# Down products of a SwiGLU block: from plain blocks to Strassen's seven products

## The chip, the cores and the metric

One core of one Trainium2 chip runs the whole block in one launch. TensorE (PE in the profile) multiplies, VectorE (DVE), ScalarE (ACT) and GpSimd (POOL) work on whole tiles, and SyncE (SP) issues the DMAs. Each engine takes its instructions in a fixed order and waits on semaphores. The metric is the device time of one execution in microseconds (us). The kernel before takes 2565.43 us, the median of 3 runs (2564.19 to 2566.57).

## The reference

One decoder block on 1024 tokens of width 1024: an input projection, sparse attention and a Mamba-2 mixer side by side, a merge with an output projection, and then a SwiGLU feed-forward of width `D_FF` = 2816, in float32. The change is in the last part:

```python
h = rms_norm(x, norm2_w[l]) * (1.0 + sc2) + sh2
x = x + gt2 * ((jax.nn.silu(h @ w_gate[l]) * (h @ w_up[l])) @ w_down[l])
return rms_norm(x, norm_f_w)
```

## The kernel before

A float32 product is made of three matmuls in a rounded format (`mm3k`, L292 to L297): every operand is split into a high part (a rounded copy, made by ACT) and a low part (operand minus high part, made by DVE or POOL), and high times high, high times low and low times high are summed in PSUM. One such step on 128 rows, 128 columns and 512 moving columns is three matmuls 128x512.

**Stages.** Startup and projections; the attention with the remaining input projections as fill between its steps (`background`, tiles `fps`); the SSD scan; the output projection; gate and up (`gate_up`, tiles `gu`); down (`down`, tiles `dps`); and the final norm. A `Flow` object (L105 to L211) sets the order at build time: each piece of work is queued with its needs and an assumed cost, and an engine takes the first of its queue whose needs are met by the assumed times. The chip then runs these orders as they are.

**Gate and up** already go by Strassen's scheme (Winograd's form, seven block products in place of eight): the tokens are cut in two halves (even and odd groups of 128), the inner width in two halves, and a block `b` of 256 columns of w_gate or w_up in two halves; there are 11 such blocks. `ff_sums` (L1814) puts the seven products of a block together on DVE; silu is ACT's, the product of gate and up POOL's (L1886), and `store_act` writes the result, 128 columns by 512 tokens, to DRAM (L1892).

**Down** runs in two halves `h` of the tokens. In each, eight PSUM banks hold the output (4 token tiles by 2 column halves), and for each of 22 slices `f` of the inner width `down_load` brings 128 rows of w_down (512 KB) and 256 KB of act, splits them (three pieces, `part`, L1693 ACT and L1695 DVE or POOL), and 8 steps of three matmuls follow: 2 x 22 x 8 = 352 steps. The w_down rows are loaded and split in both halves. Twelve pieces and 18 rows of 128x512 are shared; loads go three slices ahead. When a bank is full, DVE multiplies it by the gate vector (L1966) and adds it to the residual `x2` (L1969), ACT sums the squares (`square`, L1983), and `final` (L1987) makes the root on DVE (L1990 and the small steps L259 to L269), scales, and stores. In the second half the last three slices run bank by bank, so that the banks end one after the other:

```python
jobs = [(f, t, c) for f in range(NFF - LAST * h) for t in range(4) for c in range(2)]
if h:
    jobs += [(f, t, c) for t in range(4) for c in range(2) for f in range(NFF - LAST, NFF)]
```

Of the kernel before, what the change touches and what calls it, by code (L numbers as in the profile page):

```python
# [19 lines left out]
D = 1024  # L20
# [11 lines left out]
WD_BUFS = {"ml": 1, "x1t": 8, "sl": 1}  # L32
# [207 lines left out]
class Kern:  # L240
# [316 lines left out]
    def projections(self):  # L557
# [20 lines left out]
        self.gst = {2: [], 5: []}  # L578
        self.ck = None
# [513 lines left out]

    def load_fill(self, n):
# [8 lines left out]
    def background(self):  # L1103
# [75 lines left out]
        for n, (kd, b) in enumerate(self.order):  # L1179
# [234 lines left out]
    def tail(self):  # L1414
# [6 lines left out]
        self.actd = self.dr.tile([NFF, 128, 1024], F, name="actd")  # L1421
# [266 lines left out]
    def part(self, p, src, need, lo_eng):  # L1688
# [129 lines left out]
    def ff_sums(self, s, p, q, b, ps, op):  # L1818
# [60 lines left out]
        for m, h, nm in ready:  # L1879
# [4 lines left out]
            else:  # L1884
# [3 lines left out]
                self.store_act(g, e, 2 * b + m, h)  # L1888

    def store_act(self, g, e, f, h):  # L1890
        A, V, G, D = self.ops()
        self.acts[f][h] = e = D(0.73, [e], lambda: self.nc.sync.dma_start(self.actd[f, :, 512 * h:512 * h + 512], g.t))  # L1892
        g.until(e)

    def down_load(self, h, f):
# [3 lines left out]
        raw = self.buf("raw", [128, 2, 512], f"wd{h}{f}")  # L1899
        d = D(1.46, [raw], lambda: nc.sync.dma_start(raw.t.rearrange("p a c -> p (a c)"), self.a["w_down"][128 * f:128 * f + 128]))  # L1900
        ws = []
        k4 = lambda x: x.rearrange("p (k c) -> p k c", c=128)
        for c in range(2):
            p = self.piece()
            ws.append((p, self.part(p, lambda c=c: k4(raw[:, c]), d, "VG"[c])))
        raw.until(*[w[1] for w in ws])
        x, p = self.row(), self.piece()
        d = D(0.73, [self.acts[f][h], x], lambda: nc.sync.dma_start(x.t, self.actd[f, :, 512 * h:512 * h + 512]))
        e = self.part(p, lambda: k4(x.t), d, "V")
        x.until(e)  # L1910
        return (p, e), ws

    def down_start(self):

        self.dl = {}
        self.dnext = [(h, f) for h in range(2) for f in range(NFF)]
        self.down_more()

    def down_more(self):
        if self.dnext and self.acts[self.dnext[0][1]][self.dnext[0][0]] is not None:  # L1920
            h, f = self.dnext.pop(0)
            self.dl[h, f] = self.down_load(h, f)

    def down(self):

        nc, a = self.nc, self.a
        A, V, G, D = self.ops()
        self.x2 = x2 = self.buf("h32", [128, NT, 1024], "x2")
        gn = self.buf("h32", [128, 2, 1024], "gn")
        x2op = []  # L1930

        for h in range(2):
            self.down_more()
        g2op = D(1.46, [gn] + self.gst[5], lambda: nc.sync.dma_start(gn[:, 0], self.gtd[1]))
        nfop = D(1.46, [gn], lambda: nc.sync.dma_start(gn[:, 1], a["norm_f_w"].partition_broadcast(128)))
        LAST = 3
        for h in range(2):
            banks = {}
            for n in range(8):
                t, c = divmod(n, 2)  # L1940
                banks[t, c] = self.buf(("s", "mm", "t", "o", "s", "mm", "t", "s")[n], [128, 512], "dps")
            jobs = [(f, t, c) for f in range(NFF - LAST * h) for t in range(4) for c in range(2)]
            if h:
# [406 lines left out]
```

## Time and profile before

| | us |
|---|---|
| median of 3 runs | 2565.43 |
| profiled execution | 2557.07 |
| its span, first to last instruction | 2555.3 |
| PE busy in the span | 2467.0 (97%) |
| down: first to last `dps` matmul starts | 2294.4 to 2540.1 |
| after the last matmul, to the end of the span | about 15 |

The span is what the trace shows; what lies around it is 1.8 us. A busy PE is back to back with matmuls; an engine's idle time counts only where the PE, or at the end the last store, waits for it. Times of instructions are those of this one execution.

### The profile page before, as it was taken

How to read it: one execution, taken by the hardware profiler on the slowest of the kernel's cores; microseconds unless marked ns; L12 is line 12 of the kernel's file. 1: busy time of each engine (PE TensorE's matmuls, PEld its weight loads, DVE VectorE, ACT ScalarE, POOL GpSimd, SP SyncE). 2: the span in 40 equal slices, each digit the busy share in tenths (PEclk: the TensorE clock that was granted, in tenths of full speed). 3: DMA queues.
4: the chain of work that ended last, by engine and by line, in shares of the span. 5: the costliest groups of instructions: out<-in, count | busy, mean ns of one | idle time of the engine just before them, and what ended most of it. 6: DMA issues, size and time to landing. Idle time of an engine off the chain costs nothing. (4 is left out here: it accounts for less than half of the span.)

```text
span 2555.3 us, 39172 instructions
## 1 busy us (share of the span) xinstructions
PE 2467.0 (97%) x13806; PEld 2108.4 (83%) x13806; DVE 1698.1 (66%) x3887; ACT 1221.9 (48%) x2614; POOL 992.9 (39%) x792
## 2 busy tenths in 40 slices
PE   5999999999999999999999999999989999999997
PEld 5999879899888898988877777779968888888886
DVE  7644887877776678765477786777875555543555
ACT  4421766666556666654556446422642322323332
POOL 2111473635362636263443432101364544542222
PEclk8999999999999999999999999999999999999999
DMA  7433332213133323132456675336222322336352
GB/s 248 131 122 102 117 90 77 75 51 105 49 91 122 110 69 100 48 99 77 132 165 218 223 233 190 114 113 225 95 80 65 95 83 71 95 104 243 120 198 79
DMA packets 226261, 308.02 MB, mean 121 GB/s; under 512 B 17417, under 2 KB 151305, under 8 KB 225553
## 3 DMA queue, kind: packets, MB, share of 16 engines
q1 hardware_dynamic: 226064, 305.52, 37.4%
q8 instruction: 109, 1.79, 0.3%
q14 instruction: 88, 0.71, 0.1%
HBM read 229.83 MB, written 75.63 MB: 120 GB/s over the span
## 5 line engine op out<-in xcount | busy, mean ns | idle before, releaser
L2106 POOL TENSOR_SCALAR P<-P,sm,gate 128x640 f32<-128x640 f32 (+7 forms) x256 | 215.2, 852 | 369.3 <-DVE sm L2103 292.8
L2177 DVE TENSOR_TENSOR kv<-tp,kv 128x512 fp32r<-128x512 f32 (+1 forms) x296 | 189.5, 657 | 117.0 <-ACT kv L2176 115.5
L2176 ACT ACTIVATE kv<-tp 128x512 fp32r<-128x512 f32 (+1 forms) x296 | 164.8, 573 | 190.4 <-PE tp L2173 183.9
L2097 ACT ACTIVATE P<-P,sm 128x640 f32<-128x640 f32 (+7 forms) x256 | 186.8, 732 | 46.5 <-DVE sm L2093 43.6
L1068 PE MATMUL o<-kv 128*128 128x512 f32 x528 | 188.8, 409 | 12.7 <-DVE kv L2177 11.3
L2088 PE MATMUL S<-kv,Q 128*128 128x384 f32 (+5 forms) x768 | 182.6, 336 | 3.5 <-DVE sm L2093 3.4
L2093 DVE CUSTOM_DVE_ANT_0 P<-S,kb 128x256 f32<-128x256 f32 (+5 forms) x256 | 120.4, 494 | 59.6 <-PE tp L2173 31.4
L1827 DVE TENSOR_TENSOR ex<-ex,gu 128x512 f32<-128x512 f32 x117 | 79.0, 684 | 121.6 <-PE gu L297 110.0
L295 PE MATMUL fps<-hT_hi,whi_x 128*128 128x512 f32 x384 | 157.8, 411 | 0.0
L2173 PE MATMUL tp<-id,P 128*128 128x128 f32 x1056 | 153.2, 272 | 0.0
L1116 DVE SCALAR_TENSOR_TENSOR u<-xr,hcw,u 128x512 f32<-128x512 f32 x144 | 141.0, 980 | 16.3 <-ACT u L1119 11.4
L297 PE MATMUL fps<-hT_hi,wlo_x 128*128 128x512 f32 x384 | 150.9, 393 | 0.0
L296 PE MATMUL fps<-hT_lo,whi_x 128*128 128x512 f32 x384 | 150.7, 392 | 0.0
L295 PE MATMUL fps<-whi_z,hT_hi 128*128 128x256 f32 x512 | 150.0, 293 | 0.1
L2088 PEld LDWEIGHTS S<-kv,Q 128*128 128x128 f32 x768 | 128.5, 189 | 20.1 <-DVE sm L2093 6.0
L2173 PEld LDWEIGHTS tp<-id,P 128*128 128x128 f32 x1056 | 127.4, 140 | 21.2 <-POOL P L2106 0.2
L297 PE MATMUL fps<-whi_z,hT_lo 128*128 128x256 f32 x512 | 144.4, 282 | 0.0
L296 PE MATMUL fps<-wlo_z,hT_hi 128*128 128x256 f32 x512 | 144.3, 282 | 0.0
L1068 PEld LDWEIGHTS o<-kv 128*128 128x128 f32 x528 | 95.4, 189 | 32.5 <-DVE kv L2177 16.8
L295 PE MATMUL gu<-M,x1r 128*128 128x512 f32 x296 | 117.5, 397 | 2.9 <-ACT x1r L1693 2.9
L1695 POOL TENSOR_TENSOR x1r<-wd,x1r 128x512 fp32r<-128x512 f32 x41 | 54.8, 1337 | 168.1 <-ACT x1r L1693 161.4
L296 PE MATMUL gu<-M,x1r 128*128 128x512 f32 x296 | 117.9, 398 | 0.5 <-DVE M L1640 0.5
(427 smaller groups left out, 7766.5 us busy)
## 6 DMA issues: line engine op xcount, KB each, us to landing
wd<-w_down SPq DMA_DIRECT2D x44, 512.0 KB, 3.4
wada<-w_ada SPq DMA_DIRECT2D x40, 512.0 KB, 4.4
ac<-acd SPq DMA_DIRECT2D x32, 512.0 KB, 4.2
raw_x<-w_in SPq DMA_DIRECT2D x24, 512.0 KB, 4.3
ff<-w_gate SPq DMA_DIRECT2D x22, 512.0 KB
ff<-w_up SPq DMA_DIRECT2D x22, 512.0 KB, 5.2
actd<-ex SPq DMA_DIRECT2D x39, 256.0 KB, 3.2
ex<-actd SPq DMA_DIRECT2D x39, 256.0 KB, 6.0
```

The lines of the kernel that those rows point to most:

```text
L295: mm(ps, lh, rh, start=k == 0, stop=False)
L296: mm(ps, lh, rl, start=False, stop=False)
L297: mm(ps, ll, rh, start=False, stop=k == kt - 1)
L1068: nc.tensor.matmul(o.t.rearrange("p h q -> p (h q)"), vst(), pair()[m], start=n + m == 0, stop=n == u.total - 1 and m == 1)
L1116: nc.vector.scalar_tensor_tensor(u.t, xr[:, k:k + N2], hcw[:, ft, k:k + 1], u.t, op0=OP.mult, op1=OP.add)
L2088: mm(sp[:, :w], q, kvb.kv[:, br, r, first + c0:first + c1], start=r == 0, stop=r == 1)
L2093: nc.vector.tensor_tensor_reduce(P[:, c0:c1], sp[:, :w], k.kb[:, m0:m0 + w], scale=-1.0, scalar=sm[:, 0, h:h + 1] if p else 3.0e38, op0=OP ...
L2097: ex = A(0.26 + 0.8333e-3 * n, [mx], lambda: nc.scalar.activation(P[:, :n], P[:, :n], AF.Exp, bias=sm[:, 1, h:h + 1], scale=-1.0, accum_ou ...
L2106: nc.gpsimd.tensor_scalar(P[:, :n], P[:, :n], sm[:, 3, m:m + 1], k.gate[:, i, self.h0 + m, br + 1:br + 2], op0=OP.mult, op1=OP.mult)
L2173: nc.tensor.transpose(tp[:, h * 128:h * 128 + 128], P, k.id)
L2176: hi = A(0.064 + 0.104 * n, [op, pair], lambda: nc.scalar.activation(pair()[0][:, c], tp[:, c], AF.Copy))
L2177: lo = V(0.068 + 0.133 * n, [hi], lambda: nc.vector.tensor_sub(pair()[1][:, c], tp[:, c], pair()[0][:, c]))
```

## The change

Down is also cut in halves, in all three directions: act in four blocks for each `b` of 256 inner columns (two inner halves, two token halves), w_down in four blocks (two inner halves, two column halves). Seven products in the order 1, 2, 6, 7, 5, 4, 3 each run over 11 blocks `b` and 4 token tiles `j`: 7 x 11 x 4 = 308 steps of three matmuls. Each product has four banks; two sets of banks take turns.

The sums of blocks are made ahead. `w_sums` makes the four sums of w_down's blocks, in 22 calls beside the first 22 units of the fill in the attention (at the third of four quarters of a unit): a load of 512 KB into a `raw` buffer (two DMAs), four subtractions on POOL in place, and four stores of 128 KB to the DRAM tile `wsd`. The two `raw` buffers are those through which the fill's weights are loaded. `act_pieces` makes the four sums of act for each block in gate and up, one on POOL and three on DVE, and stores seven rows of 256 KB in place of four.

`down_load` brings one row of act (sum) and one of w_down (sum) for each product and block, 256 KB each, splits them, and may run up to five blocks ahead of the one being multiplied. For the last product, 3, POOL first multiplies the w_down row by the gate vector, so that this product's bank can be added to the residual at once. `ends` puts the products together on DVE: one ACT copy for each bank of product 1, one DVE sum for 6 and 7, three DVE steps for 2 and 4, six for 5, one for 3. Product 4 ends the odd token tiles and 3 the even ones; the scaling by the final gain is done on POOL ahead for the half rows that product 2 ends. The last four blocks of product 3 run bank by bank.

```diff
+    def w_sums(self, b, c):
...
+        raw, cs = self.buf("raw", [128, 4, 256], f"ws{b}{c}"), slice(256 * c, 256 * c + 256)
...
+        e = D(1.46, [raw], load)
...
+        for o, x, y in ((0, 1, 0), (1, 3, 1), (3, 3, 0), (2, 2, 3)):
+            e = G(0.65, [e], lambda o=o, x=x, y=y: nc.gpsimd.tensor_tensor(raw[:, o], raw[:, x], raw[:, y], op=OP.subtract))
+        e = D(1.46, [e], lambda: [nc.sync.dma_start(self.wsd[t, b, :, cs], raw[:, m]) for t, m in enumerate((2, 0, 3, 1))])
...
+                if q == 2 and n < NFF:
+                    self.w_sums(n // 2, n % 2)
...
+    def act_pieces(self, b):
...
+        s1 = add(G, [e21, e22, S1], S1, A21, A22, OP.add)
+        s3 = add(V, [e11, e21, S3], S3, A11, A21)
+        s2 = add(V, [s1, S2], S2, S1, A11)
+        s4 = add(V, [s2, S4], S4, A12, S2)
...
+            if p == 3 and n:
...
+                d = G(1.23, [d, self.g2op], lambda x=x: nc.gpsimd.tensor_tensor(x.t, x.t, self.acc[:, 9], op=OP.mult))
+            e = self.part(pc, lambda x=x: k4(x.t), d, "VG"[(n + b) % 2], True)
...
+    DOWN = (1, 2, 6, 7, 5, 4, 3)
...
+            if p == 3:
+                t, cs = 2 * j, slice(512, 1024)
+                e = V(0.6, [op, ua[j]], lambda: nc.vector.tensor_tensor(x2[:, t, cs], x2[:, t, cs], ps.t, op=OP.add), first=True)
+                ps.until(e)
+                self.square(t, 1, e)
+                self.final(t, nf, nfop)
+                return
+            h, c = {2: (0, 0), 5: (1, 1), 4: (1, 0)}[p]
...
+            e = plus([op, u[j], y], yt, src, pt)
+            if p == 5:
+                f = plus([op, ua[j], ub[j]], pa, pa, pt)
+                ps.until(e, f)
+                f = times([f], pa, pa, c)
+                ua[j] = plus([f, x2op[j // 2]], lambda: x2[:, 2 * j, cs], lambda: x2[:, 2 * j, cs], pa)
+            else:
+                ps.until(e)
+            e = times([e], yt, yt, c)
+            e = plus([e, x2op[j // 2]], xs, xs, yt)
+            y.until(e)
+            self.square(t, c, e)
...
+            if p == 4:
+                self.final(t, nf, nfop)
...
+            tail = LAST if p == 3 else 0
+            jobs = [(b, j) for b in range(NB - tail) for j in range(4)] + [(b, j) for j in range(4) for b in range(NB - tail, NB)]
+            for b, j in jobs:
...
+                if j == 0:
+                    i = n * NB + b
+                    while len(self.dl) < min(i + 6, 7 * NB):
                         self.down_more()
```

On POOL, early in the attention, the rows before stand thus (`P` is a head's softmax, scaled by its sums and gate; `xr` belongs to the fill):

```order
L1123 MEMSET xr 128x3
L2106 TENSOR_SCALAR P_0_1_3247<-P_0_1_3247,sm_0_1_3161,gate 128x128
L2106 TENSOR_SCALAR P_0_1_3249<-P_0_1_3249,sm_0_1_3161,gate 128x128
L2106 TENSOR_SCALAR P_0_1_3253<-P_0_1_3253,sm_0_1_3161,gate 128x128
L2106 TENSOR_SCALAR P_0_1_3269<-P_0_1_3269,sm_0_1_3161,gate 128x128
L2106 TENSOR_SCALAR P_1_0_3359<-P_1_0_3359,sm_1_0_3271,gate 128x256
```

And now, at the same place (L2190 is the line that was L2106, L1144 was L1123; `ws` is the raw buffer of `w_sums`):

```order
L1144 MEMSET xr 128x3
L2190 TENSOR_SCALAR P_0_1_3243<-P_0_1_3243,sm_0_1_3179,gate 128x128
L2190 TENSOR_SCALAR P_0_1_3246<-P_0_1_3246,sm_0_1_3179,gate 128x128
L2190 TENSOR_SCALAR P_0_1_3252<-P_0_1_3252,sm_0_1_3179,gate 128x128
L2190 TENSOR_SCALAR P_0_1_3262<-P_0_1_3262,sm_0_1_3179,gate 128x128
L1110 TENSOR_TENSOR ws_3371<-ws_3371 128x256 x4
L2190 TENSOR_SCALAR P_1_0_3364<-P_1_0_3364,sm_1_0_3265,gate 128x256
```

Four subtractions, which wait for their load, now stand between two groups of P; 22 such groups are spread over the attention.

On DVE, around the last splits of down, the kernel before has this (`dps` is a full bank, `x` the residual, `rq_nf` the root of a token tile; L1695 is a split):

```order
L1695 TENSOR_TENSOR wlo_pc<-ex,whi_pc 128x512
L1695 TENSOR_TENSOR x1r_19661<-wd_23837,x1r_19661 128x512
L1695 TENSOR_TENSOR wlo_pc<-ex,whi_pc 128x512
L1966 TENSOR_TENSOR ex<-dps,gn 128x512
L1969 TENSOR_TENSOR x_22616<-x_22616,ex 128x512
```

And the changed kernel has this around its last two splits (L1719 is the split, L1993 a sum of `ends`, L2089 the scaling in `final`, L2015 the first bank of product 3):

```order
L1993 TENSOR_TENSOR x_22887<-x_22887,ex 128x512
L259 TENSOR_SCALAR rq_nf_23919<-rq_nf_23919 128x1
L264 SCALAR_TENSOR_TENSOR rq_nf_23919<-rq_nf_23919 128x1
L259 TENSOR_SCALAR rq_nf_23919<-rq_nf_23919 128x1
L264 SCALAR_TENSOR_TENSOR rq_nf_23919<-rq_nf_23919 128x1
L2080 TENSOR_TENSOR rq_nf_23964<-rq_nf_23964 128x1
L2089 SCALAR_TENSOR_TENSOR x_22887<-x_22887,rq_nf_23919,acc 128x512
L1719 TENSOR_TENSOR wlo_pc<-ex,whi_pc 128x512
L1719 TENSOR_TENSOR x1r_19607<-ex,x1r_19607 128x512
L2089 SCALAR_TENSOR_TENSOR x_22887<-x_22887,rq_nf_23919,acc 128x512
L266 TENSOR_SCALAR rq_nf_23964<-rq_nf_23964 128x1
```

Before, the last splits stood ahead of the first bank's work. Now they stand behind the sums and roots that product 4 leaves: between the first sum of product 4 and the first of product 3, DVE has 65 instructions: 7 splits, 4 sums from PSUM, 8 steps from SBUF, 6 scalings of 128x512 and 40 small ones.

## Rows read from the trace of the kernel before

**Rows 1.** The page's busy time of each engine, its share of the span and its instructions.

```profile
PE 2467.0 (97%) x13806; PEld 2108.4 (83%) x13806; DVE 1698.1 (66%) x3887; ACT 1221.9 (48%) x2614; POOL 992.9 (39%) x792
```

**Rows 2.** Busy time in stretches of the span: length, then us busy (and instructions) of PE, its weight loads, DVE, ACT and POOL, the granted clock as a share of full speed, the DMA engines' busy share, and GB/s. Attention in two stretches, the second half of gate and up in one, down in two, and what comes after the last matmul.

```profile
160.00:600.00 440.00, 428.17 (x2778) 382.35 (x2777) 318.57 (x855) 249.48 (x590) 177.66 (x163) 1.00 0.29 89
600.00:1160.00 560.00, 550.26 (x3496) 490.70 (x3495) 397.82 (x948) 339.59 (x784) 277.14 (x243) 1.00 0.29 88
...
2180.00:2294.00 114.00, 114.00 (x494) 92.50 (x494) 63.44 (x77) 35.34 (x62) 54.33 (x39) 1.00 0.27 85
2294.00:2417.00 123.00, 123.00 (x531) 99.20 (x530) 48.38 (x51) 39.13 (x67) 30.22 (x24) 1.00 0.57 203
2417.00:2540.50 123.50, 123.45 (x530) 99.11 (x528) 68.53 (x124) 42.43 (x84) 32.37 (x24) 1.00 0.38 127
2540.50:2555.40 14.90, 0.00 (x0) 0.00 (x0) 10.86 (x35) 4.22 (x9) 3.79 (x3) 0.65 0.37 136
```

**Rows 3.** The first matmuls of the steps that write `dps` (L295, in three groups by where the operands lie) and the last of the third matmul (L297): count, ns shortest/median/longest, first and last start in us.

```profile
L295 PE MATMUL dps<-x1r,whi_pc x216: 394/399/400, 2328.0 to 2539.6; 128*128 128x512 f32 x108
...
L297 PE MATMUL dps<-x1r,wlo_pc x216: 390/394/397, 2328.4 to 2540.1; 128*128 128x512 f32 x108
...
L295 PE MATMUL dps<-whi_pc,x1r x68: 389/397/400, 2294.4 to 2450.0; 128*128 128x512 f32 x68
...
L295 PE MATMUL dps<-x1r,x1r x68: 387/395/398, 2295.1 to 2449.3; 128*128 128x512 f32 x68
```

**Rows 4.** What PE waited for in the attention, 160 to 1160 us: in total, times, longest. The first two of its waits.

```profile
PE o L1068 <- DVE kv L2177: 11.3, 9, 2.2
PE S L2088 <- DVE sm L2093: 3.4, 4, 1.3
```

**Rows 5.** What POOL waited for in the same stretch, the longest in total.

```profile
POOL P L2106 <- DVE sm L2103: 259.8, 35, 20.4
```

**Rows 6.** Groups of POOL instructions by shape: busy us, mean ns of one, idle before.

```profile
L1331 POOL TENSOR_TENSOR acc<-acc,wada 128x512 f32<-128x512 f32 x64 | 85.5, 1336 | 1.0
...
L2106 POOL TENSOR_SCALAR P<-P,sm,gate 128x256 f32<-128x256 f32 x32 | 21.0, 668 | 38.9 <-DVE sm L2103 22.6 <-DVE st L2133 9.0 <-PE S L2088 7.3
```

**Rows 7.** DVE in the middle of down's first half: start us, duration us, instruction. Two pairs of splits.

```profile
2383.97 0.69 DVE L1695 TENSOR_TENSOR x1r<-wd,x1r 128x512 fp32r<-128x512 f32 x1 [2.95 <-ACT x1r L1693]
2385.24 1.37 DVE L1695 TENSOR_TENSOR wlo_pc<-ex,whi_pc 128x512 fp32r<-128x512 f32 x1 [0.58 <-ACT whi_pc L1693]
```

**Rows 8.** POOL at the same time, in the same columns.

```profile
2384.77 1.30 POOL L1695 TENSOR_TENSOR x1r<-wd,x1r 128x512 fp32r<-128x512 f32 x1 [4.30 <-ACT x1r L1693]
```

**Rows 9.** Stretches of down, columns as in rows 2: its first 31 us, the 31 us behind the end of its first half, and 3 us in the load of `x2`.

```profile
2294.00:2325.00 31.00, 31.00 (x135) 24.89 (x134) 12.20 (x13) 10.38 (x18) 9.52 (x8) 1.00 0.88 320
...
2417.00:2448.00 31.00, 31.00 (x135) 25.05 (x134) 25.95 (x69) 13.42 (x31) 7.81 (x5) 1.00 0.53 163
...
2319.00:2322.00 3.00, 3.00 (x15) 2.40 (x14) 0.36 (x1) 0.13 (x1) 0.00 (x0) 1.00 1.04 427
```

**Rows 10.** Waits of ACT in down: the splits wait for a piece that PE still reads.

```profile
ACT x1r L1693 <- PE dps L297: 77.4, 22, 3.9
```

**Rows 11.** Groups of DVE instructions in down, 2294 to 2541 us: count, busy us, mean ns. A sum from PSUM, a sum from SBUF, a scaling, and two of the small steps of a root.

```profile
L1969 DVE TENSOR_TENSOR x<-x,ex 128x512 f32<-128x512 f32 x12 | 10.6, 892 | 0.1
...
L1966 DVE TENSOR_TENSOR ex<-dps,gn 128x512 f32<-128x512 f32 x12 | 8.3, 689 | 5.8 <-PE dps L297 5.8
...
L1997 DVE SCALAR_TENSOR_TENSOR x<-x,rq_nf,gn 128x512 f32<-128x512 f32 x8 | 7.7, 1003 | 0.0
...
L259 DVE TENSOR_SCALAR rq_nf<-rq_nf 128x1 f32<-128x1 f32 x15 | 3.7, 265 | 0.0
L264 DVE SCALAR_TENSOR_TENSOR rq_nf<-rq_nf 128x1 f32<-128x1 f32 x15 | 3.3, 222 | 0.0
```

**Rows 12.** DVE at the end, behind the last matmul: the last bank, the last sum of squares, the last scaling.

```profile
2544.13 0.68 DVE L1966 TENSOR_TENSOR ex<-dps,gn 128x512 f32<-128x512 f32 x1
...
2547.36 1.21 DVE L1990 TENSOR_TENSOR rq_nf<-rq_nf 128x1 f32<-128x1 f32 x1
...
2551.24 0.49 DVE L2006 TENSOR_SCALAR x<-x,rq_nf 128x512 f32<-128x512 f32 x1
```

**Rows 13.** ACT at the end: the last sum of squares and the last scaling.

```profile
2546.50 0.63 ACT L1983 ACTIVATE ex<-x 128x512 f32<-128x512 f32 x1 [1.98 <-DVE rq_nf L264]
2547.04 0.19 ACT L1983 ACTIVATION_READ_ACCUMULATOR ex<-x 128x1 f32 x1
...
2551.22 0.72 ACT L2004 ACTIVATE x<-x,rq_nf 128x512 f32<-128x512 f32 x1 [1.26 <-DVE rq_nf L264]
```

**Rows 14.** The page's DMA issues of down: KB each, median us from issue to landing.

```profile
wd<-w_down SPq DMA_DIRECT2D x44, 512.0 KB, 3.4
...
ex<-actd SPq DMA_DIRECT2D x39, 256.0 KB, 6.0
```

More of the change, by code (lines that the diff above doesn't have):

```diff
@@ L1686, in ff_raw, with part @@
         return raws
-    def part(self, p, src, need, lo_eng):
+    def part(self, p, src, need, lo_eng, first=False):
         nc = self.nc
@@ L1887, in ff_sums @@
                 x.until(e)
[L1888 to L1895, printed above, removed]
+                self.ablk[m, h] = g, e
+                if len(self.ablk) == 4:
+                    self.act_pieces(b)
+    def act_pieces(self, b):
         nc = self.nc
         A, V, G, D = self.ops()
-        raw = self.buf("raw", [128, 2, 512], f"wd{h}{f}")
-        d = D(1.46, [raw], lambda: nc.sync.dma_start(raw.t.rearrange("p a c -> p (a c)"), self.a["w_down"][128 * f:128 * f + 128]))
-        ws = []
-        k4 = lambda x: x.rearrange("p (k c) -> p k c", c=128)
[L1903 to L1911, printed above, removed]
@@ new lines, in act_pieces, with add @@
+        blk, self.ablk = self.ablk, {}
+        (A11, e11), (A12, e12), (A21, e21), (A22, e22) = (blk[k] for k in ((0, 0), (1, 0), (0, 1), (1, 1)))
+        S1, S2, S3, S4 = (self.row() for _ in range(4))
+        def add(E, need, o, x, y, op=OP.subtract):
+            eng = nc.vector if E is V else nc.gpsimd
+            return E(0.6 if E is V else 1.23, need, lambda: eng.tensor_tensor(o.t, x.t, y.t, op=op))
+        s1 = add(G, [e21, e22, S1], S1, A21, A22, OP.add)
+        s3 = add(V, [e11, e21, S3], S3, A11, A21)
@@ new lines, in act_pieces, with down_load @@
+        s2 = add(V, [s1, S2], S2, S1, A11)
+        s4 = add(V, [s2, S4], S4, A12, S2)
+        for p, r, e, more in ((1, A11, e11, [s2, s3]), (2, A12, e12, [s4]), (4, A22, e22, [s1]), (5, S1, s1, [s2]),
+                              (6, S2, s2, [s4]), (7, S3, s3, []), (3, S4, s4, [])):
+            self.acts[p, b] = d = D(0.73, [e], lambda p=p, r=r: nc.sync.dma_start(self.actd[p][b], r.t))
+            r.until(d, *more)
+        A21.until(s1, s3)
+    def down_load(self, p, b):
+        nc = self.nc
+        A, V, G, D = self.ops()
+        k4 = lambda x: x.rearrange("p (k c) -> p k c", c=128)
+        out = []
+        for n in range(2):
+            x, pc = self.row(), self.piece()
+            if n == 0:
+                src, need = (lambda: self.actd[p][b]), [self.acts[p, b]]
+            elif p < 4:
+                f, c = ((0, 0), (1, 0), (1, 1))[p - 1]
+                src, need = (lambda: self.a["w_down"][(2 * b + f) * 128:(2 * b + f) * 128 + 128, 512 * c:512 * c + 512]), []
+            else:
+                src, need = (lambda: self.wsd[p - 4, b]), self.wsop[b]
+            d = D(0.73, need + [x], lambda x=x, src=src: nc.sync.dma_start(x.t, src()))
+            if p == 3 and n:
+                d = G(1.23, [d, self.g2op], lambda x=x: nc.gpsimd.tensor_tensor(x.t, x.t, self.acc[:, 9], op=OP.mult))
+            e = self.part(pc, lambda x=x: k4(x.t), d, "VG"[(n + b) % 2], True)
+            x.until(e)
+            out.append((pc, e))
+        return out
@@ L1913, in down_start @@
     def down_start(self):
         self.dl = {}
[L1916 removed]
+        self.dnext = [(p, b) for p in self.DOWN for b in range(NFF // 2)]
         self.down_more()
     def down_more(self):
[L1920 to L1922 removed]
+        if self.dnext and self.dnext[0] in self.acts:
+            self.dl[self.dnext[0]] = self.down_load(*self.dnext[0])
+            self.dnext.pop(0)
@@ L1935, in down @@
[L1935 to L1943, printed above, removed]
-                jobs += [(f, t, c) for t in range(4) for c in range(2) for f in range(NFF - LAST, NFF)]
-            for f, t, c in jobs:
-                if (h, f, t, c) == (0, 6, 0, 0):
+        g2op = self.g2op = D(1.46, [acc] + self.gst[5], lambda: nc.sync.dma_start(
+            acc[:, 8:10].rearrange("p a c -> p (a c)"), self.gtd[1]))
```

126 lines of the change are left out of this document (73 added, 53 removed).

## The prediction

> **What bounds the kernel.** I read the busy shares first: PE is busy for 97% of the span [rows 1]. Then the stretches [rows 2]: in gate and up and in down PE has no gap at all (114.00 of 114.00, 123.00 of 123.00, 123.45 of 123.50), at a granted clock of 1.00, which is the 2.4 GHz level. In the attention, 160 to 1160 us, it is idle for 11.8 + 9.7 = 21.6 us of 1000. Behind the last matmul come 14.9 us with no PE work. So time is gained where matmuls go away, and lost where something new makes PE wait or the end grow longer. The other engines have room on average (in down DVE 39 to 55%, ACT a third, POOL a quarter), so I next read who waits for whom, and then the single instructions at the end.
>
> **Matmuls removed.** 352 steps become 308, so 44 x 3 = 132 matmuls go, all 128x512. The first and the last of down's 1056 matmuls start at 2294.4 and 2540.1 us [rows 3] (216 + 68 + 68 = 352 steps): 245.7 / 1055 = 0.233 us from one to the next. The 390 to 400 ns of a single one overlap the next and aren't the price. 132 x 0.233 = 30.7 us, and as PE is back to back before and behind, all of it comes off the end unless something new waits. Down's products then last 924 x 0.233 = 215 us.
>
> **Sums of w_down, in the attention.** 22 x 4 = 88 subtractions 128x256 on POOL. The rows have no such operation; a one-input 128x256 takes 668 ns and a two-input 128x512 takes 1336 ns, half of which is 668 [rows 6]. I take 0.7 us: 62 us of POOL, which is busy for 455 us of these 1000 [rows 2] and waited 260 us there for the softmax sums before it could scale P [rows 5]. That idle time is the cover. Two things aren't covered: the four subtractions stand in POOL's order ahead of P groups and wait for a load of 512 KB, which takes 3.4 us from issue to landing where a row shows one [rows 14]; and the order of attention steps and fill on PE shifts. PE's own waits there are few (11.3 us for the low parts of P, [rows 4]). At the bottom nothing is lost, and a lucky order gives 3 us back; 22 waits with half a P group's delay on PE make some 10 us. I take +3, near the lower end, since POOL's idle time is four times the added work. The added DMA, 22 x 1 MB in 1000 us, is 23 GB/s on 88, and the DMA engines are busy for 29% [rows 2].
>
> **Sums of act, in gate and up.** Each of 11 blocks adds three DVE steps (0.69 us alone, 1.37 beside POOL, [rows 7]) and one on POOL (1.34, [rows 6]): 23 to 45 us of DVE and 15 of POOL over some 430 us (1848 matmuls at 0.233) in which DVE is 56% and POOL 48% busy [rows 2]. Seven stores now stand together on SP behind these sums, with the next block's weight loads behind them; those weights are needed a product series (28 x 3 x 0.233 = 20 us) later. Cost 0 to 5 us; I take 1.
>
> **Loads of down.** Each block needs 512 KB in 12 x 0.233 = 2.8 us, or 188 GB/s; before, the first 31 us moved 320 GB/s with PE full, and 427 were reached [rows 9]. The 4 MB of `x2` hold the queue for some 10 us; the loads behind it are five blocks, 14 us, ahead, and splits today wait for pieces rather than for data [rows 10]. The first blocks are loaded while gate and up end. I take 1 us, bounds 0 and 8.
>
> **Splits and the end.** Pieces fall from 3 for 5.6 us to 2 for 2.8 us: with 0.69 to 1.37 us for the half that goes to DVE, one in each 2.8 us is no bound while nothing else runs there. Something does. Behind product 5 DVE has 24 steps (17 to 27 us) and behind product 4 the sums and roots. From the first sum of product 4 to the first bank of product 3 PE needs (28 + 4) x 3 x 0.233 = 22.4 us, and DVE has 65 instructions. At the price of the stretch behind the first half of the old down, 25.95 us for 69 [rows 9], that is 24.4 us. There POOL worked only 7.81 of 31 us; now it has two operations of 1.3 us in each 2.8 us (multiply and split). A two-input DVE step that meets one takes 1.37 instead of 0.69: in the pair of rows POOL ran from 2384.77 to 2386.07 and DVE's split from 2385.24 on ended 0.54 us after it [rows 7, 8]. With all 21 such steps at 1.37, 4 from PSUM at 0.69 and 40 small ones at 0.22 [rows 11] it is 28.8 + 2.8 + 8.8 = 40.4 us. I take 30, as POOL is busy most of that time but not always in the way. The last two splits, for blocks 9 and 10, stand behind about 80% of this list, so are ready at 24, where PE wants them at 21: PE stalls for 3 us (0 to 12).
>
> Behind the last matmul the chain is now shorter: one sum (0.69), the squares (0.63 + 0.19), a root (2.3: three pairs at 0.27 + 0.22 and four more small steps at no more than 0.22, [rows 11]), a scaling (0.7) and the store, which with the rest took 3.4 us from 2551.94 [rows 12, 13]: 8 us, with small gaps some 10, in place of 14.9. But the four banks come each 2.8 us, and DVE has about 3 us of work for each and starts some 8 us late, of which the stall absorbs 3; I give 4 of the 5 saved back. The end as a whole: +3 - 5 + 4 = +2, bounds -5 and +10.
>
> On these collisions the Trainium skill is stricter than my middle value ("SBUF — State Buffer", Who interferes with whom): a DVE instruction with two SBUF inputs and a GpSimd instruction that reads SBUF take the same port, and the later one blocks until the other ends. The two rows on the pair agree with it. By that rule alone, with POOL always busy, the list takes its upper 40 us and the end comes at the first rival below.
>
> **Sum.** -30.7 + 3 + 1 + 1 + 2 = -23.7 us. The profiled execution took 2557.07 us, 1.8 around its span; the median of the runs lies 8.4 above it, which no term explains and which I leave as it is: 2565.43 - 23.7, about 2541.
>
> **Rivals.**
> *DVE and POOL bound the last products.* For it: 40 us of DVE against 22, and before this POOL's 22 operations of product 3 take 22 x 1.3 = 29 us of the 36 that they have. Against it: the old first half's end had the same density without a PE wait. PE then stalls for about 12 instead of 3 us, and the end gains nothing: 2541 + 9 + 4 = 2554.
> *Nothing new waits.* For it: PE's waits of 2.2 us and less in the attention, and splits that wait for PE. Then -30.7 - 5 and nothing else: 2530.
> *Slower: the sums of w_down stand in the attention's way.* Mechanism: P's scaling, the transposes and the products of P with V hang on POOL in order; 88 subtractions of 0.7 us put 62 us in front of them. For it: POOL alone scales P, and the waits in rows 4 are on that path. Against: 260 us in which POOL waited for P's sums. It decides from 24 us on, that is when more than 38% of the 62 us reach PE; with all, 2541 - 3 + 62 = 2600.
> *No change* would need these 24 us from several places at once, or seven products that PE doesn't run back to back, for instance 0.077 us more for each of the 308 steps because loads lag throughout: 2565.
>
> **How the numbers follow.** Forecast, 2534 to 2549: 0.62. DVE and POOL at the end, about 2554: 0.17. Nothing waits, about 2530: 0.12. No change: 0.05. Slower by the attention: 0.04. The range of 8 in 10 leaves out the far rivals and half of the nearest: 2528 to 2556. What a measurement of this kernel can tell from no change is about 0.2%, or 5 us; below 2560.3 is faster: 0.62 + 0.17 + 0.12 = 0.91. Same 0.05, slower 0.04.
>
> **What would show it.** 924 `dps` matmuls 0.233 us apart, over 215 to 219 us, show the first term right; more than 222 shows that down starves, and the wait on PE names the cause: a DMA for the loads, DVE or POOL splits near the end for the collisions. PE idle in 160 to 1160 us of 20 to 30 shows the third part right, above 45 wrong. Product 3's first sum on DVE should come late by some 8 us, and the stretch behind the last matmul should be 10 to 15 us. The forecast is wrong if PE's gaps in down exceed 8 us, or if the attention grows by more than 10.

## The result and the profile after

The changed kernel takes 2542.54 us, the median of 4 runs (2537.87 to 2546.49), beside 2566.0 us (4 runs, 2564.19 to 2569.66) for the kernel before: a ratio of 0.9906, 95% interval 0.9886 to 0.9926, which is 24 us (19 to 29) less. The forecast was 2541, with a range of 2528 to 2556.

The busy times of the page after, which answer to [rows 1]: PE has 132 matmuls fewer and 27.3 us less work, POOL 139 instructions and 176 us more, DVE 106 us more.

```profile
PE 2439.7 (96%) x13674; PEld 2082.0 (82%) x13674; DVE 1803.7 (71%) x3937; ACT 1238.7 (49%) x2640; POOL 1169.3 (46%) x931
```

The stretches after, in the columns of [rows 2]: the attention in two parts, the second half of gate and up less a little, the first 31 us of down, 31 us of its fifth and sixth products, and the end.

```profile
160.00:600.00 440.00, 425.83 (x2751) 379.95 (x2750) 315.98 (x848) 248.94 (x587) 199.84 (x193) 1.00 0.36 107
600.00:1160.00 560.00, 550.41 (x3496) 489.53 (x3496) 407.43 (x952) 341.38 (x785) 326.66 (x300) 1.00 0.37 113
2185.00:2302.00 117.00, 117.00 (x506) 94.74 (x505) 78.19 (x85) 35.24 (x61) 66.12 (x45) 1.00 0.33 111
2302.00:2333.00 31.00, 31.00 (x136) 25.09 (x134) 13.17 (x13) 9.98 (x16) 17.78 (x12) 1.00 0.92 327
2455.00:2486.00 31.00, 31.00 (x135) 25.02 (x135) 31.00 (x32) 10.87 (x22) 20.04 (x13) 1.00 0.44 135
2500.00:2510.00 10.00, 8.12 (x33) 5.47 (x31) 10.00 (x25) 2.98 (x7) 8.70 (x6) 1.00 0.01 2
2510.00:2517.00 7.00, 0.73 (x2) 0.30 (x2) 6.89 (x20) 0.89 (x3) 1.58 (x2) 0.71 0.54 179
2517.00:2524.00 7.00, 4.78 (x12) 3.41 (x13) 6.72 (x15) 1.50 (x3) 3.06 (x2) 0.56 0.32 121
2524.00:2531.50 7.50, 7.29 (x32) 5.53 (x30) 6.62 (x27) 2.91 (x7) 0.00 (x0) 1.00 0.38 141
```

The attention lost little: PE is idle for 14.2 + 9.6 = 23.8 us of the 1000, against 21.6. The second half of gate and up, which makes sums of act too, and the first products have no gap. Then a column changes that few readers would look at, as PE is still full: from 2455 us on DVE is busy 31.00 of 31.00 us with only 32 instructions, nearly 1 us for each. PE pays some 50 us later: in 2510 to 2517 it works 0.73 of 7 us, and in the 7 us behind that the granted clock is 0.56, close to the lower level of 1.2 GHz.

Down itself: groups of `dps` steps as in [rows 3], the earliest first start and the latest last one, and below what PE waited for in down (line; us in total, times, longest).

```profile
L295 PE MATMUL dps<-whi_pc,x1r x48: 387/394/400, 2302.1 to 2497.3; 128*128 128x512 f32 x48
L297 PE MATMUL dps<-x1r,wlo_pc x156: 389/392/628, 2305.4 to 2530.9; 128*128 128x512 f32 x156
```

```profile
PE dps L295 <- ACT x1r L1717: 6.8, 1, 6.8
PE dps L296 <- DVE x1r L1719: 2.2, 3, 1.3
PE dps L296 <- POOL x1r L1719: 1.4, 1, 1.4
PE dps L296 <- POOL wlo_pc L1719: 0.5, 1, 0.5
```

Down lasts 228.8 us, where 924 matmuls at 0.233 us are 215, and behind the last matmul 9.6 us are left of the span (2540.5) instead of 15.2 (2555.3 - 2540.1, [rows 3]). So the matmuls that went away were worth more than the gain, and some 13 us were lost again in the last product. The experiments are about these 13 us.

### The profile page after: what moved, and what is told of

It reads as the page before. It is cut to its first block, busy times and chain, and to the rows that moved or that the text cites. A ratio compares the mean times of both kernels' runs of the same rounds, so it can differ in the third digit from the quotient of the medians.

```text
span 2540.5 us, 39589 instructions
## 1 busy us (share of the span) xinstructions
PE 2439.7 (96%) x13674; PEld 2082.0 (82%) x13674; DVE 1803.7 (71%) x3937; ACT 1238.7 (49%) x2640; POOL 1169.3 (46%) x931
## 5 line engine op out<-in xcount | busy, mean ns | idle before, releaser
L2190 POOL TENSOR_SCALAR P<-P,sm,gate 128x640 f32<-128x640 f32 (+7 forms) x256 | 215.2, 851 | 247.1 <-DVE sm L2187 186.6
L2177 DVE CUSTOM_DVE_ANT_0 P<-S,kb 128x256 f32<-128x256 f32 (+5 forms) x256 | 120.5, 495 | 56.7 <-PE tp L2257 29.5
L1137 DVE SCALAR_TENSOR_TENSOR u<-xr,hcw,u 128x512 f32<-128x512 f32 x144 | 150.2, 1043 | 13.3 <-ACT u L1140 8.3
L295 PE MATMUL fps<-hT_hi,whi_x 128*128 128x512 f32 x384 | 157.3, 410 | 0.1
L1717 ACT ACTIVATE x1r<-ex 128x512 fp32r<-128x512 f32 x147 | 89.7, 627 | 135.4 <-POOL ex L1736 31.2
L297 PE MATMUL fps<-hT_hi,wlo_x 128*128 128x512 f32 x384 | 151.0, 393 | 0.0
L295 PE MATMUL fps<-whi_z,hT_hi 128*128 128x256 f32 x512 | 149.8, 293 | 0.1
L1719 DVE TENSOR_TENSOR x1r<-ex,x1r 128x512 fp32r<-128x512 f32 x102 | 122.6, 1213 | 33.3 <-ACT x1r L1717 33.0
L297 PE MATMUL fps<-whi_z,hT_lo 128*128 128x256 f32 x512 | 144.4, 282 | 0.0
L2331 POOL TENSOR_TENSOR dx<-xs,hd 128x512 f32<-128x512 f32 x32 | 43.4, 1355 | 170.2 <-DVE yy L2373 127.9
```

The lines of the kernel that those rows point to most:

```text
L295: mm(ps, lh, rh, start=k == 0, stop=False)
L297: mm(ps, ll, rh, start=False, stop=k == kt - 1)
L1137: nc.vector.scalar_tensor_tensor(u.t, xr[:, k:k + N2], hcw[:, ft, k:k + 1], u.t, op0=OP.mult, op1=OP.add)
L2190: nc.gpsimd.tensor_scalar(P[:, :n], P[:, :n], sm[:, 3, m:m + 1], k.gate[:, i, self.h0 + m, br + 1:br + 2], op0=OP.mult, op1=OP.mult)
```

## The experiments

In all of them "down" is the time from the first to the last start of a `dps` matmul and "end" what the span has behind that, both from the profiled execution; the ratio is to the kernel before, timed on the same chip. A single execution lies up to 10 us off its median (the kernel before took 2558.32 us once beside a median of 2568.65), and ahead of down two traces of one kernel differ by several us (the kernel before starts down at 2294.4 us in one and 2301.6 in the other). Down and end repeat better: 260.9 us in both traces of the kernel before, 238.4 and 238.0 in those of the changed one. So the column "down + end" tells causes better than the span.

| kernel | median us (runs) | ratio [95%] | down | end | down + end |
|---|---|---|---|---|---|
| `c_before` | 2564.26 (1) | | 245.6 | 15.3 | 260.9 |
| `c_after` | 2546.31 (6) | 0.9915 [0.990, 0.993] | 228.4 | 9.6 | 238.0 |
| `no_wsums` | 2545.84 (6) | 0.9914 [0.9898, 0.993] | 228.3 | 9.8 | 238.1 |
| `no_mult` | 2532.69 (5) | 0.9865 [0.9848, 0.9882] | 216.1 | 11.1 | 227.2 |
| `loads_first` | 2547.41 (5) | 0.9924 [0.9908, 0.9939] | 230.9 | 9.4 | 240.3 |
| `early` | 2544.21 (5) | 0.991 [0.9894, 0.9926] | 224.3 | 9.9 | 234.2 |
| `dve_mult` | 2542.44 (5) | 0.9922 [0.9906, 0.9937] | 227.4 | 9.4 | 236.8 |
| `bank_mult` | 2534.54 (4) | 0.9872 [0.9854, 0.9889] | 216.0 | 12.6 | 228.6 |
| `bank_mult_b` | 2534.13 (4) | 0.9883 [0.9869, 0.9897] | 216.0 | 12.5 | 228.5 |
| `bank_early` | 2534.82 (4) | 0.9889 [0.9874, 0.9903] | 214.8 | 12.5 | 227.3 |
| `bank_pre` | 2537.18 (4) | 0.9894 [0.9878, 0.9911] | 217.8 | 10.9 | 228.7 |
| `bank_early_loads` | 2541.88 (4) | 0.9904 [0.9886, 0.9922] | 222.2 | 10.8 | 233.0 |

The kernel before took 2568.65 us (11 runs) beside the first four, 2566.1 (9) beside `loads_first`, `early`, `bank_mult` and `bank_early_loads`, and 2564.74 (9) beside the rest.

### Which added work costs something: the two kernels again, and each addition left out

`c_before` and `c_after` are the two kernels unchanged.

> The kernel before once more, on the chip on which the other three of this call run, so that stages are compared on one chip. The trace read for the prediction came from an execution of 2557 us, 9 us under the median of its runs. If that was another chip or an unusual execution, this one takes about 2566 us, and the 9 us show in the stages ahead of down (SSD, attention); if the stages are the same to 1 us, the 9 us lie around the span.

> The changed kernel as it is, beside the kernel before on the same chip: 2542 us, about 24 us under it. By the theory that down alone decides, its stages ahead of down are within 5 us of the kernel before, down takes 229 us in place of 246, and the stretch behind the last matmul 9.5 in place of 15. By the rival (the sums of w_down cost much in the attention) down starts 8 us later or more than in the kernel before, as the two traces at hand show it.

`no_wsums` makes no sums of w_down:

```diff
-                if q == 2 and n < NFF:
-                    self.w_sums(n // 2, n % 2)
...
-                src, need = (lambda: self.wsd[p - 4, b]), self.wsop[b]
+                src, need = (lambda: self.a["w_down"][256 * b:256 * b + 128, 0:512]), []
```

> Leaves out the sums of w_down in the attention (loads, 88 subtractions on POOL, stores); products 4 to 7 read plain rows of w_down in their place, so loads and splits in down stay. If the sums cost what the forecast took (3 us, between -3 and 10), it takes 2536 to 2542. If the 62 us of POOL stand in the attention's way for the 8 us by which down starts later in the trace at hand, it takes 2534 and down starts at about 2294. If a reordered attention was luck, it is slower than the changed kernel.

`no_mult` makes no multiplication of w_down's rows by the gate in product 3:

```diff
             if p == 3 and n:
-                d = G(1.23, [d, self.g2op], lambda x=x: nc.gpsimd.tensor_tensor(x.t, x.t, self.acc[:, 9], op=OP.mult))
+                pass
```

> Leaves out POOL's multiplication of the w_down rows of product 3 by the gate vector (11 steps). The trace of the changed kernel shows PE waiting some 10 us for splits near the end of product 3. Theory A, DVE's queue (31.0 of 31 us busy in product 4, from the ends of product 5 on): DVE keeps its steps and only meets POOL less often, so 6 us or more of the wait stay and it takes 2536 to 2541. Theory B, POOL's chain of multiply and split: the wait goes, and it takes about 2531.

The sums of w_down are free within what can be measured: 0.5 us less without them, and the same 238 us of down and end; by the intervals a cost of some 5 us could still hide. The multiplications cost 13.6 us, nearly as much as the 11 x 1.3 us of POOL's work, though POOL is idle for a third of the time there (20.04 us busy of 31, above), and without them down takes its 216 us. Without them the stall is gone. What the run doesn't tell is how they make it. Its time is near that of theory B, but POOL's chain alone isn't the cause: `dve_mult` (below) takes the multiplications off POOL, and PE still waits. `Flow` also sets the orders anew for each kernel, so what a run says of a change includes the new orders.

The kernel before, traced again, came to 2562.5 us of span, and the 7.2 us over the first trace are there before down begins (2301.6 against 2294.4). That is most of the 8.4 us by which the first profiled execution lay under its median. In `c_after` down starts at 2307.1 us, 5.5 later than in `c_before`: more than the 5 of the theory that down alone decides, less than the 8 of its rival. `no_wsums` still starts it at 2305.3, so the sums explain at most 2 of the 5.5; the rest isn't explained and is no more than two traces of the kernel before differ by.

What DVE and POOL do meanwhile in `c_after` (start, duration, instruction), 17 us before PE stops:

```profile
2497.87 1.19 DVE L1993 TENSOR_TENSOR x<-x,ex 128x512 f32<-128x512 f32 x1
2498.98 1.79 DVE L1996 TENSOR_TENSOR ex<-ex,acc 128x512 f32<-128x512 f32 x1
2500.69 0.67 DVE L1993 TENSOR_TENSOR ex<-acc,dps 128x512 f32<-128x512 f32 x1
...
2514.59 1.25 DVE L264 SCALAR_TENSOR_TENSOR rq_nf<-rq_nf 128x1 f32<-128x1 f32 x1
2515.76 1.40 DVE L2089 SCALAR_TENSOR_TENSOR x<-x,rq_nf,acc 128x512 f32<-128x512 f32 x2
```

```profile
2496.76 1.75 POOL L1719 TENSOR_TENSOR x1r<-ex,x1r 128x512 fp32r<-128x512 f32 x1
2498.47 1.76 POOL L1956 TENSOR_TENSOR ex<-ex,acc 128x512 f32<-128x512 f32 x1
2500.17 1.75 POOL L1719 TENSOR_TENSOR x1r<-ex,x1r 128x512 fp32r<-128x512 f32 x1
...
2514.55 1.27 POOL L1956 TENSOR_TENSOR ex<-ex,acc 128x512 f32<-128x512 f32 x1
2522.04 1.27 POOL L1956 TENSOR_TENSOR ex<-ex,acc 128x512 f32<-128x512 f32 x1 [6.21 <-DMA ex<-w_down]
```

The engines take turns. With both queues full, a POOL step of 1.27 us shows as 1.75 and a DVE step with two SBUF inputs of 0.68 shows as 1.79; a DVE step that reads one input from PSUM (`ex<-acc,dps`) keeps its 0.67 beside a POOL step. Even a DVE step of one column (L264, 0.15 us alone) lasts 1.25 us, from 2514.59 to 2515.84, when POOL's of 2514.55 ends at 2515.82. This is what the Trainium skill says ("SBUF — State Buffer", Who interferes with whom): the later of the two blocks until the other ends. So DVE gets one such step done in 1.7 us instead of 0.7 (the `x2` row: two in 1.40, with POOL at rest), and all that needs DVE falls behind.

### What PE waits for at last: loads, DVE's queue, or a port

The trace of `c_after` offers a simple cause. POOL's last multiplication waited 6.21 us for a row of w_down (above), and SP's queue shows why the row was late:

```profile
2495.67 0.33 SPq L1953 DMA_DIRECT2D ex<-w_down  x1
2516.53 1.00 SPq L2092 DMA_DIRECT2D out<-x  x2
2517.62 0.41 SPq L1953 DMA_DIRECT2D ex<-actd  x1
2518.09 0.46 SPq L1953 DMA_DIRECT2D ex<-w_down  x1
```

SP stood 20 us in front of two output stores that wait for DVE's final scaling (L2089 at 2515.76), with the last block's loads behind them. Three kernels test this and its rivals. `loads_first` puts these loads ahead of the stores:

```diff
-                    while len(self.dl) < min(i + 6, 7 * NB):
+                    while len(self.dl) < min(i + (8 if n == 6 else 6), 7 * NB):
```

> The changed kernel with one number altered: in product 3 the loads run 8 blocks ahead instead of 6, so the last block's two loads stand on SP ahead of product 4's first two output stores instead of behind them; nothing else is left out or added. Theory SP (the output stores, which wait for DVE's late final scaling, hold the last loads back; POOL then waits 6.2 us for the row and PE 7.2 us): PE's long wait in the down stage goes to under 2 us, the half-clock matmuls behind it go too, and the time falls by 6 to 9 us against the changed kernel as timed beside it (2546): 2537 to 2540. Theory queue (the multiplications and splits on POOL are late by themselves, whatever SP does): the wait only changes its name to a split on POOL or DVE, under 2 us gained, 2544 to 2546.

The loads alone aren't it: 2547.41 us, nothing gained. The last loads leave before 2500 us now, yet PE waits 10.9 us until 2514.19, again for a split on ACT. ACT in `loads_first` (start, duration, what it waited for), and below three rows of ACT in `c_after`:

```profile
2509.61 0.63 ACT L2073 ACTIVATE ex<-x 128x512 f32<-128x512 f32 x1 [4.54 <-DVE rq_nf L267]
...
2512.89 0.63 ACT L2073 ACTIVATE ex<-x 128x512 f32<-128x512 f32 x1 [1.53 <-DVE x L1993]
2513.43 0.19 ACT L2073 ACTIVATION_READ_ACCUMULATOR ex<-x 128x1 f32 x1
2513.52 0.61 ACT L1717 ACTIVATE x1r<-ex 128x512 fp32r<-128x512 f32 x1
```

```profile
2520.35 0.63 ACT L2073 ACTIVATE sl<-x 128x512 f32<-128x512 f32 x1 [8.04 <-DVE x L1993]
...
2521.39 0.63 ACT L1717 ACTIVATE whi_pc<-ex 128x512 fp32r<-128x512 f32 x1 [0.32 <-DMA ex<-actd]
2521.92 0.61 ACT L1717 ACTIVATE x1r<-ex 128x512 fp32r<-128x512 f32 x1
```

The splits stand in ACT's order behind squares (L2073) of tiles that DVE hasn't summed yet. In `c_after` both queues stood still for DVE: SP in front of the loads, and ACT for 8.04 us in front of the splits. The split that PE waited 7.2 us for is the last row, and of the time in front of it the late load explains only the 0.9 us from 2521.07, where the square ends, to 2521.92. SP's wait was a real row and at most a small part of the cause: without it, ACT's wait for the same late engine was there. The run isn't a clean test of the loads, since the longer lead that it gives them costs something itself (`bank_early_loads`, below).

`early` moves work of DVE ahead: the shares gate x pa and gate x pb are added to `x2` at the ends of products 6 and 7, so each tile has three steps in place of six at the end of product 5 (and four more before it, one more in all).

```diff
             if p == 6:
                 ua[j] = plus([op, ua[j]], pa, pa, pt)
                 ps.until(ua[j])
+                xa[j] = share([ua[j]], 2 * j, pa)
                 return
...
             if p == 5:
-                f = plus([op, ua[j], ub[j]], pa, pa, pt)
...
+                e = times([op, y], yt, pt, c)
...
+                ua[j] = plus([e, xa[j]], lambda: x2[:, 2 * j, cs], lambda: x2[:, 2 * j, cs], yt)
+                e = plus([e, xb[j]], xs, xs, yt)
...
```

> The changed kernel with DVE's steps at product 5's ends cut from six per tile to three: the gate times pa and the gate times pb are made and added to x2 already at the ends of products 6 and 7; the same output. POOL's multiplication in product 3 stays. Theory backlog (DVE is late with the final scaling because the steps of product 5's ends have queued up on it since 2455): the output stores leave about 8 us earlier, the last loads with them, PE's long wait shrinks to under 2 us, and the time falls by 5 to 9 us to 2537 to 2541. Theory exclusion (DVE is late because its two-input steps take 1.2 to 1.8 us instead of 0.69 while POOL multiplies, in product 3 itself): under 3 us gained, 2543 to 2546.

Median 2544.21, a ratio of 0.991 against 0.9915 for `c_after`: within the intervals nothing. Its traced execution, the fastest of its five, has down at 224.3 us, 4 less, and the intervals allow as much. There DVE comes to product 4's first bank in time, having waited for PE, while in `c_after` (second row) it does so 4.4 us later, counted from the start of down:

```profile
2485.63 0.69 DVE L1993 TENSOR_TENSOR ex<-acc,dps 128x512 f32<-128x512 f32 x1 [1.06 <-PE dps L297]
```

```profile
2493.86 0.67 DVE L1993 TENSOR_TENSOR ex<-acc,dps 128x512 f32<-128x512 f32 x1
```

From then on DVE is full again, and PE still waits 5.4 us for a split on ACT. So DVE's backlog from product 5 is worth some 4 us of the stall, in this one trace, and moving work ahead of product 3 is no cure. `dve_mult` leaves the work and changes the engine:

```diff
-                d = G(1.23, [d, self.g2op], lambda x=x: nc.gpsimd.tensor_tensor(x.t, x.t, self.acc[:, 9], op=OP.mult))
+                d = V(0.6, [d, self.g2op], lambda x=x: nc.vector.tensor_tensor(x.t, x.t, self.acc[:, 9], op=OP.mult))
```

> The changed kernel with product 3's 11 multiplications by the gate moved from POOL to DVE, on the same rows in SBUF; the same output, nothing left out. DVE has 11 steps of 0.69 us more, 7.6 us, in a stretch in which it is never idle. Theory exclusion (what makes DVE late is that its steps with two SBUF inputs take 1.2 to 1.8 us while POOL multiplies; some twelve of them lose about 1.1 us each, 13 us): without POOL's multiplications DVE loses less than it takes on, the waits of PE in product 3 shrink from 10 us to 2 to 6, and the time is 2536 to 2542. Theory work (DVE is simply given too many steps, whatever POOL does): its queue grows by 7.6 us, the waits to 14 us or more, and the time is 2549 to 2554.

2542.44 us and 0.9922, as much as `c_after` (0.9915) within the intervals: the 7.6 us of added DVE work cost next to nothing, so theory work as put is out. But the time lies just above the range of theory exclusion too, and PE's waits, 9.5 us, are well above its 2 to 6. Each has a part in it; how much, no run tells apart. DVE's groups in `dve_mult`, 2480 to 2526 us (count, busy us, mean ns), the multiplications first:

```profile
L1956 DVE TENSOR_TENSOR ex<-ex,acc 128x512 f32<-128x512 f32 x11 | 8.4, 780 | 0.0
L1993 DVE TENSOR_TENSOR x<-x,ex 128x512 f32<-128x512 f32 x4 | 2.7, 681 | 0.0
L1996 DVE TENSOR_TENSOR ex<-ex,acc 128x512 f32<-128x512 f32 x4 | 3.8, 954 | 0.0
```

and the groups of the last two in `c_after`, 2490 to 2536 us:

```profile
L1996 DVE TENSOR_TENSOR ex<-ex,acc 128x512 f32<-128x512 f32 x4 | 4.9, 1231 | 0.0
L1993 DVE TENSOR_TENSOR x<-x,ex 128x512 f32<-128x512 f32 x5 | 4.9, 974 | 0.0
```

With POOL lighter DVE's steps are shorter (974 to 681 and 1231 to 954 ns), which pays for the eleven new ones: from 147.9 to 213.9 us behind the start of down, DVE gets 69 instructions of 128x512 done, and 57 in `c_after`. But the splits of ACT now wait for multiplications in DVE's full queue (PE's longest wait is 9.0 us).

### Fewer steps, and a better kernel

If DVE and POOL together are too slow by what eleven multiplications cost, the cure is to have fewer. `bank_mult` multiplies product 3's four finished banks by the gate, out of PSUM, in place of eleven rows of w_down:

```diff
-            if p == 3 and n:
-
-                d = G(1.23, [d, self.g2op], lambda x=x: nc.gpsimd.tensor_tensor(x.t, x.t, self.acc[:, 9], op=OP.mult))
...
-                e = V(0.6, [op, ua[j]], lambda: nc.vector.tensor_tensor(x2[:, t, cs], x2[:, t, cs], ps.t, op=OP.add), first=True)
+                y = self.row()
+                e = times([op, y], lambda: y.t, pt, 1)
                 ps.until(e)
+                e = plus([e, ua[j]], lambda: x2[:, t, cs], lambda: x2[:, t, cs], lambda: y.t)
...
```

> The changed kernel without POOL's 11 multiplications of w_down rows by the gate; instead DVE multiplies each of product 3's four finished banks by the gate, out of PSUM, and adds it then: the same output, four more DVE steps of about 0.69 us, one of them at the very end. Both theories of the gap in product 3 expect what leaving the multiplication out gave, plus one step at the end: 2533 to 2535. If the bank's steps at the end queue up behind the final scalings on DVE, the stretch behind the last matmul grows by 2 to 3 us and the time is 2536 to 2537.

> bank_mult once more, beside the other three on one chip: 0.987 of the time before, as the first time (0.9854 to 0.9889).

2534.54 us (0.9872) and, once more on another chip, 2534.13 (0.9883): 0.2 to 0.4% or 6 to 11 us under the changed kernel (0.9906 and 0.9915), and of the kernels that leave nothing out none is faster. What PE waited for in the whole of down, in `bank_mult`:

```profile
PE dps L296 <- POOL x1r L1719: 0.9, 1, 0.9
PE dps L295 <- ACT x1r L1717: 0.2, 1, 0.2
```

SP still stands in front of the output stores there, from 2490 to 2504.29 us, and it costs nothing: counted from the start of down the stores leave 9 us earlier (200.5 us against 209.4), and the loads behind them too. A comparison of the two kernels over 66 us that begin 147.9 us behind the start of down in each, first `c_after`, then `bank_mult` (columns of [rows 2]):

```profile
2455.00:2521.00 66.00, 58.07 (x247) 45.53 (x245) 62.06 (x87) 24.64 (x51) 44.46 (x28) 0.98 0.37 113
```

```profile
2451.70:2517.70 66.00, 64.97 (x278) 51.93 (x278) 61.40 (x108) 27.16 (x56) 28.29 (x19) 1.00 0.43 136
```

DVE is nearly full in both, and its busy time, which counts the time blocked, is about the same; but it gets 108 instructions done instead of 87.

Three kernels tried to add to it. `bank_early_loads` is `bank_mult` with the changes of `early` and `loads_first`; `bank_early` leaves the loads as they were; `bank_pre` lets POOL multiply by the final gain the half rows that product 5 ends, for ACT to scale at the end, instead of four scalings on DVE:

```diff
-            if p == 2:
-                self.pre[t] = G(1.23, [self.sq[t][0], nfop], ...
+            if p != 4:
+                self.pre[t, c] = G(1.23, [self.sq[t][c], nfop], ...
...
```

> All three together: bank multiplication on DVE, product 5's share made early, loads 8 blocks ahead in product 3; the same output. Left in the down stage: 924 matmuls at 0.233 us, 215 to 216 us, and 8 to 11 us behind the last. If bank_mult alone already has no gap, the other two add only 0 to 3 us through an earlier end of the final scalings: 2530 to 2535.

> bank_mult with DVE's steps at product 5's ends made early, and the loads as in the changed kernel; the same output. It tells which of the two additions cost bank_early_loads 7 us against bank_mult. If the longer lead of the loads did it (it puts splits of later blocks ahead of what is due on POOL, ACT and DVE): 2533 to 2536, as bank_mult. If the early steps did it: 2540 to 2543.

> bank_mult with one half of the final scaling of four tiles taken from DVE: POOL multiplies the half rows that product 5 ends by the final gain, ACT scales them at the end; the same output. DVE has four steps of 0.70 us fewer in its full stretch, POOL four of 1.3 us more ahead of it, ACT four of 0.72 us more. If DVE's queue still sets the end: 1 to 3 us less than bank_mult, 2531 to 2534. If ACT's splits now wait behind scalings that wait for DVE, PE waits again and it is 2536 to 2542.

None is better. `bank_early` equals `bank_mult` (0.9889 and 0.9883), so the early shares are worth nothing once the stall is gone. `bank_early_loads` missed its forecast of 2530 to 2535: it lost 7 us against `bank_mult` on the same chip. They come with the longer lead of the loads, the one thing that `bank_early` leaves out (down 214.8 us against 222.2, on two chips): in its trace PE waits 3.8 us for a split on DVE and 1.3 for one on ACT. It agrees with `loads_first`, which was no faster either. That loads taken earlier put splits in front of work that is due sooner is the likely reason; no run shows it by itself. `bank_pre` has a shorter end (10.9 us against 12.5) and pays it back with 2.0 us for a split on ACT; its median of 2537.18 isn't told from `bank_mult_b` by the intervals.

## Why the prediction was right, and where it wasn't

The time came out 1.5 us from the forecast, and that is in part luck: one term was too small by 9 us, and four others were too large by some 9 together. By parts, from `c_before` and `c_after` except where said:

- **Matmuls removed, -30.7.** Right. Without the stall down takes 216.1 us (`no_mult`) against 245.6, which is -29.5, and 1.2 us of waits are left in it.
- **Sums of w_down in the attention, +3 (-3 to 10).** Of no measurable size: 0.5 us by `no_wsums`, PE idle 23.8 us against 21.6 (first two traces). The cover that was named held: POOL waited 158 us for the softmax sums instead of 260 [rows 5]. A subtraction took 0.85 us and not the 0.7 that was taken:

```profile
POOL P L2190 <- DVE sm L2187: 158.2, 34, 12.7
L1110 POOL TENSOR_TENSOR ws<-ws 128x256 f32<-128x256 f32 x88 | 74.9, 852 | 38.1 <-issue 17.2 <-DMA ws<-w_down 16.1 <-POOL xr L1144 0.9
```

- **Sums of act, +1, and loads of down, +1.** Right in size: both next to nothing. From the first `gu` to the first `dps` matmul before takes 441.8 us (2294.4 - 1852.6) and after 441.9 (2302.1 - 1860.2). Soon behind the load of `x2` PE waited 0.5 us once (`wlo_pc`, above; not in `c_after`), and the first 31 us at 327 GB/s had PE full.
- **Splits and the end, +2.** This is the step that failed, in two terms that partly cancel each other. The stall was put at 3 us (0 to 12); it is 12.3 us of down (228.4 - 216.1), of which 9.4 are waits (10.6, less the 1.2 of `no_mult`) and most of the rest is the clock (below). The end was put at -5 with 4 given back, on the ground that DVE would come to product 3's banks 8 us late; it is -5.7 (15.3 to 9.6). In `no_mult`, where PE has no such gap, the end is 11.1 us: the gap lets DVE work off its list and shortens the end by 1.5 us, and without it DVE is some 3 us late for the first bank, not 8. Together stall and end are +6.6 instead of +2.

The sum of the measured parts, -29.5 + 0.5 + 0 + 6.6, is about -22, beside -22.3 between the medians of that chip (2546.31 and 2568.65).

Why was the stall mis-sized? The list of 65 instructions and a price of a collision were there. In `c_after` the list runs from the row at 2493.86 above to this one:

```profile
2528.01 0.68 DVE L2015 TENSOR_TENSOR x<-x,dps 128x512 f32<-128x512 f32 x1
```

These are 34.1 us, where 30 was taken and 40 was the upper bound (in `no_mult` they are 27.0). The middle value of 30 took POOL for a worker who is "not always in the way". The rows of before on which it leaned were pairs that met once, at 1.37 [rows 7, 8]; with both queues full a step can meet a whole POOL step, at 1.79. So the upper bound, with 1.37 for every step, wasn't the most that the blocking could cost; the 21 steps came to 1.10 us in the mean, as POOL had no work for part of the time. The prediction took this bound for the rule of the Trainium skill worked out; by the rule ("SBUF — State Buffer", Who interferes with whom) a step that comes second waits for the whole of the other, as the rows at 1.79 show. The other part is DVE's backlog: the list began 4.4 us later than in `early`, where DVE waited for the bank and down was 4 us shorter. The prediction counted the steps behind product 5 and put no delay for them. It also treated only the splits of blocks 9 and 10 as late, by DVE's own order, and didn't look at what else stands behind DVE: ACT's squares ahead of ACT's splits.

So the first rival, DVE and POOL bound the last products, was the true course of the stall (12 us, as it said) and wrong about the end, which it held to gain nothing. "Nothing new waits" fell in down but was right for the attention. The sign that was named for a wrong forecast, gaps in down of over 8 us, did appear, while the time stayed: a sum can be right with several of its terms wrong, and only the rows tell.

## What to carry to other kernels

Before work is put on an idle POOL, look at what DVE does in the same microseconds, and price each DVE step with two SBUF inputs at a whole POOL step for as long as both queues are full (1.7 us here), not at that of pairs that happen to meet; where POOL runs out of work the price falls back to 0.7. Where a factor can be taken on a few finished banks out of PSUM instead of on every row that goes in, it is fewer steps: 4 here in place of 11. When PE starves and the trace names a DMA or ACT, follow the wait back to the engine that is never idle; a queue that is merely in front of it can be cleared without any gain.

## What was not expected of the hardware

Two things. The exclusion reaches to two-input instructions of one column, as the row of L264 above shows: 1.25 us in place of 0.15. And a gap on PE costs more than its length. Matmuls in `c_after` around the long wait (start, duration, what PE waited for):

```profile
2514.98 0.39 PE L297 MATMUL dps<-x1r,wlo_pc 128*128 128x512 f32 x1
2522.59 0.79 PE L295 MATMUL dps<-x1r,x1r 128*128 128x512 f32 x1 [7.21 <-ACT x1r L1717]
2524.51 0.80 PE L296 MATMUL dps<-x1r,x1r 128*128 128x512 f32 x1 [1.13 <-DVE x1r L1719]
...
2526.38 0.63 PE L297 MATMUL dps<-x1r,wlo_pc 128*128 128x512 f32 x1
2526.81 0.63 PE L295 MATMUL dps<-x1r,whi_pc 128*128 128x512 f32 x1
...
2528.06 0.39 PE L295 MATMUL dps<-x1r,whi_pc 128*128 128x512 f32 x1
2528.29 0.39 PE L296 MATMUL dps<-x1r,whi_pc 128*128 128x512 f32 x1
```

Behind the wait of 7.2 us the matmuls come 0.43 us apart instead of 0.23, at a granted clock of 0.50, the level of 1.2 GHz, until 2528.06. Between 2522.59 and there stand nine matmuls; at 0.233 they would take 2.1 us, they took 5.5, of which 1.1 is a wait, so the clock added some 2.2 us to the stall. In the runs without a long gap (`bank_mult`, `bank_early`) no such stretch was seen: the granted clock there is 1.00 over the last 30 us of down.
